# The adaLN sums of a two-layer trunk block: from VectorE and TensorE to ScalarE and GpSimd

## The chip, the core and the metric

The kernel runs on one NeuronCore of a Trainium2 chip. The metric is the device time of one execution in microseconds (us). TensorE is PE in the rows, its weight loads PEld, VectorE is DVE, ScalarE is ACT, GpSimd is POOL, and SyncE is SP, which issues all the loads.

## The reference, cut to what matters

Two trunk layers, each with a mixer sub-layer (two attentions and a pooling branch) and a squared-ReLU MLP, run on 256 latent and 256 context tokens of width 1024. Each layer takes its shifts, scales and gates from two conditioning vectors:

```python
def modulate(x, g, shift, scale):
    return rmsnorm(x, g) * (1 + scale) + shift

def adaln(v, w, b):
    m = jax.nn.silu(v) @ w + b          # v: 1024, w: 1024 x 6144
    return jnp.split(m, 6, axis=-1)     # shift, scale, gate of each sub-layer
...
x = x + g1 * merge(oa, ob, oc, ga, gb, gc, w_br_a[l], w_br_b[l], w_br_c[l], w_out[l])
x = x + g2 * mlp(modulate(x, norm2[l], sh2, sc2), w_mlp1[l], w_mlp2[l])
```

The change concerns the product `silu(v) @ w` alone. Layer 0 needs it for both vectors; layer 1 needs it for both in the first norm and for the latents' vector alone after that.

## The kernel before

All numbers are float32. To keep their precision on TensorE, every operand is split into a high part (a cast on ScalarE) and a low part (a subtraction on VectorE), and a product takes three matmuls (`mm3`). The weights come as pieces `st` of 128 x 1024 values; `halves` turns a piece into `wh` and `wl`, each in one of four buffers (`W_HL_BUFS`), ahead of its use. Each engine runs its own queue of instructions in a fixed order. The order comes from a planner: cooperative threads (`_Flow`) emit the program, and a table of assumed costs (`_Engine`, `_TensorEngine`) tells each thread when to go on.

The first norm's shift and scale in layer 0 are made on TensorE at the start (`First`), and the change leaves that alone. The other adaLN sums are a background thread, `ada_all`. It walks over groups of 512 of the 6144 columns. For each group `ada_acc` loads eight 128 x 512 tiles of the weights (`sta`, two tiles to a load) and, for each vector, multiplies each tile by a silu column `s_col` (one value per partition) and adds it to an accumulator `acc`. This is one instruction on VectorE for each tile and vector. What is left is a sum over the 128 partitions, for 32 accumulators in all:

- shift and scale (`ada_cols_end`, 20 accumulators): four transposes on TensorE into the tile `act`, then a reduction on VectorE gives columns (`mod`);
- gates (`ada_rows_end`, 12 accumulators): `acc` is split into `ach` and `acl`, two matmuls with a matrix of ones give the sum on every partition (`ar`), and VectorE adds it to the loaded bias `grow`.

GpSimd has little to do before: the powers of the norms (`rstd`, `qr`, `rsqA`, `rsqC`), the rotary tables `tab` and a few memsets.

Of the kernel before, what the change touches and what calls it, by code (L numbers as in the profile page):

```python
# [9 lines left out]
F32R = mybir.dt.float32r  # L10
AF = mybir.ActivationFunctionType
# [4 lines left out]
P = 128  # L16
# [18 lines left out]
ADA_PAUSE = 0.8  # L35
# [8 lines left out]
ADA_SLACK = 10.0  # L44
# [7 lines left out]
# order in which the layers take the chunks of w_in (see _layout)  # L52
# [6 lines left out]
# the loads of the start: token tiles, halves of the first norm's shift and scale, halves of the first chunks  # L59
# [11 lines left out]
class _Event:  # L71
    """A point of the program whose results other threads wait for."""
# [5 lines left out]
class _Engine:  # L78
    """An engine whose instructions advance the flow's estimate of its time table."""
# [58 lines left out]
class _TensorEngine:  # L138
# [6 lines left out]
    def _step(self, out, lhsT, rhs, size, transpose=False):  # L145
        """the array's clock is full in a tick after one with enough columns, else half"""
# [27 lines left out]
class _Flow:  # L174
    """Cooperative threads that emit the program in the order in which the tensor engine should run it.

    A thread yields None (it can go on at once), a time (it can go on then) or an event."""
# [26 lines left out]
    def ready(self, *aps, eng=None):  # L204
        """when an engine sees the last write to these regions"""
# [21 lines left out]
    def held(self, pool):  # L227
        """how many tiles of a pool are in use"""
# [4 lines left out]
    def free(self, *aps):  # L233
        """the last uses of these tiles are in the program"""
# [8 lines left out]
    def room(self, pool, n, most):  # L243
        """wait until n more tiles of a pool fit"""
# [44 lines left out]
# priorities of the threads, the lowest number first  # L289
# [4 lines left out]
def kernel(ctx: ExitStack, tc: tile.TileContext, a: dict, out: bass.AP):  # L294
# [55 lines left out]
    def stage(src, nk, ncol):  # L350
        """a load of at most 1024 columns, on its way"""
# [14 lines left out]
    def halves(v, nk, ncol):  # L366
        """(hi, lo) of a staged load's rows"""
# [13 lines left out]
    class Chunk:  # L381
        """the (hi, lo) pairs of a chunk's rows, in two pieces"""
# [12 lines left out]
        def used(self, k):  # L395
            """row k is not needed any more, nor are those before"""
# [3 lines left out]
    class Stream:  # L400
        """Chunks of weights [128, nk, ncol], each staged in two loads and split ahead of its use"""
# [24 lines left out]
        def next(self):  # L426
            """the next chunk"""
# [5 lines left out]
    def mm3(ps, lh, rh, start, stop):  # L433
        """ps (+)= (lh_hi + lh_lo)^T (rh_hi + rh_lo), without lo * lo"""
# [13 lines left out]
    class Pair:  # L448
        """a (hi, lo) pair of tiles that some thread is going to write"""
# [19 lines left out]
    def reload_x():  # L469
        """the stream's input for the first residual sum"""  # L470
# [14 lines left out]
    # silu(c) as columns: 0.5 c (1 + tanh(c / 2))  # L485
# [9 lines left out]
    # adds the (hi, lo) rows of both vectors  # L495
# [14 lines left out]
    def finish_mod(l, which, vec, half):  # L510
        """A = norm (1 + scale), B = shift as per-partition columns"""
# [5 lines left out]
    class First:  # L517
        """half of the columns of shift and scale of layer 0, norm 1, both vectors, on the tensor engine"""
# [6 lines left out]
        def row(self, typ, kk, w):  # L525
            """one of the eight row tiles of one type: rows (hi, lo) x vectors"""
# [37 lines left out]
    def ada_acc(l, j, vecs, accs):  # L564
        """per-partition partial sums of silu(c) @ w_ada[:, 512 j : 512 j + 512]"""
# [4 lines left out]
        nxt = yield from fetch(0)  # L570
        for h in range(4):
# [4 lines left out]
            if h == 0:  # L576
                yield from fl.room("b", len(vecs), B_BUFS - ADA_SPARE)
# [1340 lines left out]
```

## Time and profile before

| | before |
|---|---|
| median of 3 runs (lowest to highest) | 1159.73 us (1159.59 to 1160.59) |
| the profiled execution, its span | 1159.7 us |
| PE busy | 1138.5 us, 98% |
| DVE busy | 872.7 us, 75% |
| ACT busy | 636.2 us, 55% |
| POOL busy | 70.7 us, 6%, 84 instructions |

Busy time is the time in which an engine has an instruction running, over the whole span. A share near 100% says that the engine hardly ever waited; a low share says nothing of the moments in which others waited for that engine.

### The profile page before, as it was taken

The page shows a single profiled execution, that of the slowest core. Times are in us where ns is not written, and L with a number is a line of the kernel's source. Part 1 is how long each engine was busy: PE and PEld are TensorE (multiplying, and loading weights), DVE is VectorE, ACT ScalarE, POOL GpSimd, SP SyncE. Part 2 cuts the span into 40 slices and gives each one's busy share as a digit, 9 for nine tenths or more (in the row PEclk, how much of TensorE's full clock was granted, in tenths as well). Part 3 has the DMA queues.
Part 4 walks back from the last instruction along what each step waited for, and adds up shares of the span by engine and source line. Part 5 has one row for each costly group of instructions (what it writes and reads, how often), then busy time and mean ns, then how long its engine had stood idle before and what let it go on. Part 6 is the DMA issues. An engine that isn't in the chain of part 4 may idle for free.

```text
span 1159.7 us, 17946 instructions
## 1 busy us (share of the span) xinstructions
PE 1138.5 (98%) x6636; PEld 998.0 (86%) x6636; DVE 872.7 (75%) x1653; ACT 636.2 (55%) x1356; POOL 70.7 (6%) x84
## 2 busy tenths in 40 slices
PE   5999999999999999999999999989999999999998
PEld 2898889888888898888888888889999998999886
DVE  5878989889888679878677634689777885987453
ACT  6867786664633564321133323576877865666332
POOL 0224001100000000000000000023002000000000
PEclk9899999999999999999999999999999999999999
DMA  8752235243435435556655423554334471775562
GB/s 308 271 166 97 85 105 188 90 153 121 136 137 178 138 119 178 180 180 214 213 178 185 163 92 107 166 168 153 103 128 137 155 241 40 269 238 183 192 216 75
DMA packets 59992, 186.85 MB, mean 161 GB/s; under 512 B 7296, under 2 KB 8064, under 8 KB 59904
## 3 DMA queue, kind: packets, MB, share of 16 engines
q1 hardware_dynamic: 59904, 185.71, 47.8%
q8 instruction: 52, 0.85, 0.3%
q14 instruction: 36, 0.29, 0.1%
HBM read 184.63 MB, written 1.05 MB: 160 GB/s over the span
## 4 chain that ended last, share of the span: by engine, by line
PE 95%; DMA 2%; ACT 2%; DVE 1%; SPq 0%; issue 0%; POOL 0%; DVEq 0%; POOLq 0%
PE tm L167 28%; PE h L167 23%; PE g L167 17%; PE qkv L167 8%; PE br L167 6%; PE sc L167 3%; PE po L167 2%; PE pT L171 2%; PE u L167 1%; DMA ad<-in_wada_dram 1%; PE xT L171 1%; PE ada L167 1%; PE act L171 1%; PE qT L171 1%; PE kT L171 1%; ACT hh L133 1%
## 5 line engine op out<-in xcount | busy, mean ns | idle before, releaser
L133 DVE TENSOR_TENSOR wl<-st,wh 128x1024 fp32r<-128x1024 f32 x216 | 263.6, 1223 | 133.7 <-ACT wh L133 133.1
L133 ACT CAST wh<-st 128x1024 fp32r<-128x1024 f32 x216 | 227.9, 1058 | 231.8 <-PE tm L167 151.2
L167 PE MATMUL h<-hh,wh 128*128 128x256 f32 (+1 forms) x736 | 186.7, 316 | 0.0
L167 PE MATMUL h<-hh,wl 128*128 128x256 f32 (+1 forms) x512 | 168.8, 330 | 0.2 <-DVE wl L133 0.2
L133 DVE SCALAR_TENSOR_TENSOR acc<-sta,s_col,acc 128x512 f32<-128x512 f32 x224 | 159.3, 743 | 3.0 <-DMA sta<-in_wada_dram 2.4
L167 PE MATMUL tm<-wh,ah 128*128 128x512 f32 x384 | 150.3, 391 | 0.0
L167 PE MATMUL tm<-wl,ah 128*128 128x512 f32 x384 | 149.5, 389 | 0.0
L167 PE MATMUL tm<-wh,al 128*128 128x512 f32 x384 | 149.5, 389 | 0.0
L167 PE MATMUL g<-hh,wh 128*128 128x512 f32 (+1 forms) x384 | 132.6, 345 | 0.0
L167 PEld LDWEIGHTS h<-hh,wh 128*128 128x128 f32 x736 | 124.1, 190 | 8.8
L167 PE MATMUL g<-hl,wh 128*128 128x512 f32 (+1 forms) x384 | 129.3, 337 | 0.0
L167 PE MATMUL g<-hh,wl 128*128 128x512 f32 (+1 forms) x384 | 129.3, 337 | 0.0
L167 PE MATMUL h<-hl,wh 128*128 128x512 f32 (+1 forms) x288 | 105.4, 366 | 0.1
L167 PEld LDWEIGHTS h<-hh,wl 128*128 128x128 f32 x512 | 97.0, 190 | 9.3 <-DVE wl L133 0.5
L167 PEld LDWEIGHTS tm<-wh,al 128*128 128x128 f32 x384 | 72.1, 188 | 15.2
L167 PEld LDWEIGHTS tm<-wl,ah 128*128 128x128 f32 x384 | 72.1, 188 | 14.7
L167 PEld LDWEIGHTS tm<-wh,ah 128*128 128x128 f32 x384 | 72.1, 188 | 14.5
L167 PE MATMUL qkv<-wh,hh 128*128 128x256 f32 x272 | 79.7, 293 | 1.1 <-ACT hh L133 1.1
L167 PE MATMUL qkv<-wl,hh 128*128 128x256 f32 x272 | 79.0, 290 | 1.8 <-DVE wl L133 1.8
L167 PEld LDWEIGHTS g<-hh,wl 128*128 128x128 f32 x384 | 72.8, 190 | 8.0
L167 PE MATMUL qkv<-wh,hl 128*128 128x256 f32 x272 | 79.1, 291 | 0.1
L167 PEld LDWEIGHTS g<-hh,wh 128*128 128x128 f32 x384 | 72.8, 190 | 6.7 <-ACT p L133 0.3
(188 smaller groups left out, 2178.6 us busy)
## 6 DMA issues: line engine op xcount, KB each, us to landing
st<-in_w_dram SPq DMA_DIRECT2D x136, 512.0 KB, 4.5
sta<-in_wada_dram SPq DMA_DIRECT2D x80, 512.0 KB, 4.1
st<-in_win_dram SPq DMA_DIRECT2D x72, 512.0 KB, 4.6
ad<-in_wada_dram SPq DMA_DIRECT2D x32, 256.0 KB, 7.1
st<-in_wout_dram SPq DMA_DIRECT2D x8, 512.0 KB, 5.5
wor<-in_wout_dram SPq DMA_DIRECT2D x16, 256.0 KB, 4.9
grow<-in_b_ada_dram SPq DMA_DIRECT2D x12, 256.0 KB, 5.1
kr<-in_wbr_a_dram SPq DMA_DIRECT2D x12, 256.0 KB, 5.0
```

What stands on the lines that cost most here:

```text
L133: return fn(*args, **kw)
L167: return self._e.matmul(out, lhsT, rhs, start=start, stop=stop)
L171: return self._e.transpose(out, in_, identity)
```

## The change

The adaLN partial sums move. For each tile and vector ScalarE multiplies the tile by the silu column into a tile `part` (the first one straight into `acc`), and GpSimd adds `part` to `acc`. There are two `part` tiles for each vector of a group, used in turn. The sum over partitions becomes one GpSimd instruction, `partition_all_reduce`, which leaves the total on every partition (`tot`). For columns GpSimd then multiplies `tot` by the identity and VectorE reduces each row of the product to one value; for gates GpSimd adds `tot` to the bias. The factor 0.5 of one gate moves into the residual sum. The thread waits for ScalarE's and GpSimd's planned queues instead of VectorE's, and `calm_way` waits at most 12 planned us. The rest of the diff takes out comments and docstrings and is not shown.

```diff
-ADA_PAUSE = 0.8
+ADA_DEPTH = 3.0
...
+            if op == "partition_all_reduce":
+                per, cost = 6.3e-3, 0.4
...
-        while self.norms:
+        end = self.now + 12.0
+        while self.norms and self.now < end:
             yield self.now + 0.1
...
             if h == 0:
-                yield from fl.room("b", len(vecs), B_BUFS - ADA_SPARE)
+                yield from fl.room("b", 3 * len(vecs), B_BUFS - ADA_SPARE)
                 accs.extend(tmp(s="acc") for _ in vecs)
+                for i in range(2):
+                    parts[i] = [tmp(s="part") for _ in vecs]
             for k in range(2):
                 kk = 2 * h + k
-                yield from V.calm(ADA_CALM[l])
+                yield from S.calm(ADA_CALM[l])
+                yield from G.calm(ADA_DEPTH)
                 yield from fl.calm_way()
-                for acc, vec in zip(accs, vecs):
-                    sc = s_col[:, kk, vec : vec + 1]
-                    if kk == 0:
-                        V.tensor_scalar(out=acc, in0=st[:, k], scalar1=sc, scalar2=None, op0=ALU.mult)
-                    else:
-                        V.scalar_tensor_tensor(out=acc, in0=st[:, k], scalar=sc, in1=acc, op0=ALU.mult, op1=ALU.add)
+                to = parts[kk % 2] if kk else accs
+                for part, vec in zip(to, vecs):
+                    S.activation(part, st[:, k], AF.Copy, scale=s_col[:, kk, vec : vec + 1])
                 if k:
                     free(st)
-                yield fl.ready(*accs) + ADA_PAUSE
+                if kk:
+                    for acc, part in zip(accs, to):
+                        yield fl.ready(part)
+                        G.tensor_tensor(out=acc, in0=acc, in1=part, op=ALU.add)
+        free(*[q for r in parts.values() for q in r])
...
+    def ada_sum(acc):
+
+        yield fl.ready(acc)
+        yield from fl.calm_way()
+        yield from fl.room("b", 1, B_BUFS - ADA_SPARE)
+        tot = tmp(s="tot")
+        G.partition_all_reduce(tot, acc, P, ReduceOp.add)
+        yield fl.ready(tot)
+        return tot
+
     def ada_cols_end(l, which, vecs, half, typ, accs, left):
...
-            yield from banks(1, 2)
-            pt = bank("act")
-            for i in range(4):
-                PE.transpose(pt[:, i * P : (i + 1) * P], acc[:, i * P : (i + 1) * P], ident)
-            yield fl.ready(pt)
+            tot = yield from ada_sum(acc)
+
+            dg = acc.rearrange("p (i q) -> p i q", i=4)
+            G.tensor_tensor(out=dg, in0=tot.rearrange("p (i q) -> p i q", i=4), in1=ident.unsqueeze(1).to_broadcast([P, 4, P]), op=ALU.mult)
+            free(tot)
+            yield fl.ready(acc)
+            yield from V.calm(ADA_CALM[l])
             dst = mods[l][:, 2 * which + typ, vec, half * 4 : half * 4 + 4]
-            V.tensor_reduce(out=dst, in_=pt.rearrange("p (i q) -> p i q", i=4), axis=AX.X, op=ALU.add)
+            V.tensor_reduce(out=dst, in_=dg, axis=AX.X, op=ALU.add)
...
-        for (ah, al), vec, g in zip(hl, vecs, gs):
-            yield from banks(1, 2)
-            ps = bank("ar")
-            PE.matmul(ps, ones, ah, start=True, stop=False)
-            PE.matmul(ps, ones, al, start=False, stop=True)
...
+        for acc, vec, g in zip(accs, vecs, gs):
+            tot = yield from ada_sum(acc)
+            free(acc)
+            yield fl.ready(g)
+            G.tensor_tensor(out=g, in0=g, in1=tot, op=ALU.add)
+            free(tot)
```

The change also moves instructions in the fixed orders. GpSimd's queue in the attention of layer 0 held only the powers of the query and key norms before:

```order
L133 TENSOR_TENSOR rsqA_179<-rsqA_179,neg_half 128x4 x2
L133 TENSOR_TENSOR rsqA_179<-rsqA_179,neg_half 128x2
L133 TENSOR_TENSOR rsqC_180<-rsqC_180,neg_half 128x2
L133 TENSOR_TENSOR rsqA_179<-rsqA_179,neg_half 128x2
L133 TENSOR_TENSOR rsqC_180<-rsqC_180,neg_half 128x2
L133 TENSOR_TENSOR qr_2428<-qr_2428,neg_half 128x2
```

At the same place, GpSimd's queue of the changed program ends the first two accumulators of a gate:

```order
L135 TENSOR_TENSOR rsqC_172<-rsqC_172,neg_half 128x2
L135 TENSOR_TENSOR acc_766<-acc_766,part_768 128x512
L135 TENSOR_TENSOR acc_767<-acc_767,part_769 128x512
L135 TENSOR_TENSOR acc_766<-acc_766,part_770 128x512
L135 TENSOR_TENSOR acc_767<-acc_767,part_771 128x512
L135 ISA
L135 ISA tot_1533<-acc_766 128x512
L135 ISA
L135 TENSOR_TENSOR grow_1523<-grow_1523,tot_1533 128x512
L135 ISA
L135 ISA tot_1608<-acc_767 128x512
L135 ISA
```

The row that writes `tot` is the sum over partitions. The ISA rows without operands are not in the source: the built program names each one a reload of a library index, 1 ahead of the sum and 0 behind it. Over the whole program there are 32 sums and 61 reloads, one of which (index 0, ahead of the mask that makes `ident`) stands in the program before as well.

ScalarE's queue in the MLP of layer 0 held casts of the weights (`wh`) and the activations of the hidden units before:

```order
L133 ACTIVATE relu_5608<-h_1299_5550 128x512
L133 ACTIVATE ah_5618<-relu_5608 128x512
L133 CAST wh_5629<-st_5479 128x1024
L133 CAST wh_5650<-st_5541 128x1024
L133 ACTIVATE relu_5658<-h_1308_5604 128x512
L133 ACTIVATE ah_5663<-relu_5658 128x512
```

Now products for the adaLN sums stand between them:

```order
L135 ACTIVATE part_5558<-sta_5583,s_col 128x512
L135 ACTIVATE part_5559<-sta_5583,s_col 128x512
L135 ACTIVATE relu_5692<-h_1320_5645 128x512
L135 ACTIVATE ah_5697<-relu_5692 128x512
L135 ACTIVATE part_5560<-sta_5583,s_col 128x512
L135 ACTIVATE part_5561<-sta_5583,s_col 128x512
L135 CAST wh_5712<-st_5549 128x1024
L135 CAST wh_5732<-st_5637 128x1024
```

The tiles `part_5558` to `part_5561` belong to one group and are written again and again in turn, so each write stands behind GpSimd's add that read the tile's last content.

## Rows read from the trace of the kernel before

**Rows 1.** The page, part 1: busy us, share of the span, instructions.
```profile
PE 1138.5 (98%) x6636; PEld 998.0 (86%) x6636; DVE 872.7 (75%) x1653; ACT 636.2 (55%) x1356; POOL 70.7 (6%) x84
```

**Rows 2.** The page, part 4: the chain that ended last, by engine.
```profile
PE 95%; DMA 2%; ACT 2%; DVE 1%; SPq 0%; issue 0%; POOL 0%; DVEq 0%; POOLq 0%
```

**Rows 3.** Three stretches: busy us (count) of PE, PEld, DVE, ACT, POOL; clock, DMA share, GB/s.
```profile
0.00:107.00 107.00, 94.89 (x562) 76.30 (x563) 82.86 (x215) 75.69 (x220) 29.23 (x42) 0.95 0.66 226
107.00:606.00 499.00, 498.68 (x2620) 426.22 (x2620) 413.50 (x753) 247.39 (x507) 12.01 (x12) 1.00 0.45 150
606.00:1160.00 554.00, 544.94 (x3458) 495.50 (x3456) 376.30 (x687) 313.15 (x629) 29.45 (x30) 1.00 0.48 158
```

**Rows 4.** Groups by line and shape: TensorE's adaLN work. xcount | busy us, mean ns
```profile
L171 PE MATMUL act<-ident,acc 128*128 128x128 f32 x80 | 12.0, 272 | 0.0
...
L167 PE MATMUL ar<-ach,ones1.0_112 128*128 128x512 f32 x6 | 2.4, 396 | 0.0
...
L167 PE MATMUL ar<-acl,ones1.0_112 128*128 128x512 f32 x6 | 2.4, 392 | 0.0
```

**Rows 5.** The same view: VectorE's adaLN sums, a ScalarE product of the same size.
```profile
L133 DVE SCALAR_TENSOR_TENSOR acc<-sta,s_col,acc 128x512 f32<-128x512 f32 x224 | 159.3, 743 | 3.0 <-DMA sta<-in_wada_dram 2.4
...
L133 ACT ACTIVATE p<-p,den 128x512 f32<-128x512 f32 x48 | 32.5, 736 | 0.3 <-DVE den L133 0.3
```

**Rows 6.** Timeline of POOL at the start: start us, us, instruction.
```profile
0.73 0.20 POOL masks.py:197 MEMSET ident<- 128x128 f32 x1 [0.29 <-POOLq L1907]
1.01 0.29 POOL masks.py:199 TENSOR_SCALAR_AFFINE_SELECT ident<-ident 128x128 f32<-128x128 f32 x1
1.39 0.19 POOL L133 TENSOR_TENSOR pair_sum<-ident 128x2 f32<-128x2 f32 x1
```

**Rows 7.** The rotary tables' tile: ns of one, lowest/median/highest.
```profile
L133 POOL TENSOR_TENSOR tab<-rope,gains x8: 717/918/1717, 44.3 to 766.3; 128x256 f32<-128x256 f32 x8
```

**Rows 8.** Timelines of DVE and POOL about the two runs of table instructions.
```profile
43.30 0.88 DVE L133 TENSOR_SCALAR xh<-st,rstd 128x512 f32<-128x512 f32 x2 [0.44 <-POOL rstd L133]
44.27 3.69 POOL L133 TENSOR_TENSOR tab<-rope,gains 128x256 f32<-128x256 f32 x4 [1.00 <-DMA gains<-in_gains_dram]
47.38 0.17 DVE L133 TENSOR_TENSOR mod<-adat,b_col 128x8 f32<-128x8 f32 x1 [2.06 <-PE adat L167]
...
762.75 1.22 DVE L133 TENSOR_TENSOR wl<-st,wh 128x1024 fp32r<-128x1024 f32 x1
763.22 4.79 POOL L133 TENSOR_TENSOR tab<-rope,gains 128x256 f32<-128x256 f32 x4
763.89 1.84 DVE L133 TENSOR_SCALAR xh<-x,rstd 128x512 f32<-128x512 f32 x2
765.65 1.75 DVE L133 TENSOR_TENSOR wl<-st,wh 128x1024 fp32r<-128x1024 f32 x1
```

**Rows 9.** Timeline of POOL: powers of one and of four columns.
```profile
9.05 0.55 POOL L133 TENSOR_TENSOR rstd<-rstd,neg_half 128x1 f32<-128x1 f32 x1 [7.15 <-DVE rstd L133]
74.77 1.01 POOL L133 TENSOR_TENSOR rsqA<-rsqA,neg_half 128x4 f32<-128x4 f32 x1 [7.32 <-ACT v L133]
```

**Rows 10.** DMA issues: KB of one, us from issue to landing.
```profile
ad<-in_wada_dram SPq DMA_DIRECT2D x32, 256.0 KB, 7.1
...
gains<-in_gains_dram SPq DMA_DIRECT2D x1, 256.0 KB, 6.6
...
s_raw<-in_cc_dram SPq DMA_DIRECT2D x1, 8.0 KB, 1.6
...
sink<-in_sink_dram SPq DMA_DIRECT2D x1, 6.0 KB, 6.0
pscale<-in_pscale_dram SPq DMA_DIRECT2D x1, 2.0 KB, 5.4
```

**Rows 11.** Who waited for whom: us in total, times, longest us.
```profile
ACT wh L133 <- PE tm L167: 151.2, 55, 9.0
```

**Rows 12.** Groups by line and shape: one matmul of the MLP's second product.
```profile
L167 PE MATMUL tm<-wh,ah 128*128 128x512 f32 x384 | 150.3, 391 | 0.0
```

More of the change, by code (lines that the diff above doesn't have):

```diff
@@ L5 @@
 from concourse import mybir
+from concourse.bass_isa import ReduceOp
 from concourse.masks import make_identity
@@ L43 @@
 MAIN_SPARE = (1, 0)
-ADA_SLACK = 10.0
 BR_SPARE = (4, 8)
@@ L570, in ada_acc @@
         nxt = yield from fetch(0)
+        parts = {}
         for h in range(4):
@@ L627, with ada_rows @@
             rows_ev[l, i] = _Event()
-    def ada_rows(l, idx, vecs, ones, factor):
+    def ada_rows(l, idx, vecs):
         left = [0, 1]
@@ L634, in ada_rows, with ada_rows_end @@
             yield from ada_acc(l, idx * 2 + half, vecs, accs)
-            fl.spawn(ada_rows_end(l, idx, vecs, ones, factor, half, accs, left), P_ADA)
-    def ada_rows_end(l, idx, vecs, ones, factor, half, accs, left):
+            fl.spawn(ada_rows_end(l, idx, vecs, half, accs, left), P_ADA)
+    def ada_rows_end(l, idx, vecs, half, accs, left):
         yield from fl.room("grow", len(vecs), GROW_BUFS)
@@ L645, in ada_rows_end @@
             load(g, a["b_ada"][l : l + 1, c0 : c0 + 512].to_broadcast([P, 512]))
-        hl = []
-        yield from fl.room("b", 2 * len(accs), B_BUFS - ADA_SPARE)
-        for acc in accs:
-            yield from fl.calm_way()
-            ah, al = tmp(F32R, "ach"), tmp(F32R, "acl")
-            yield from hilo_steps(acc, ah, al)
-            hl.append((ah, al))
-            free(acc)
-        yield fl.ready(*[q for p in hl for q in p]) + ADA_SLACK
-        for (ah, al), vec, g in zip(hl, vecs, gs):
-            yield from banks(1, 2)
-            ps = bank("ar")
-            PE.matmul(ps, ones, ah, start=True, stop=False)
-            PE.matmul(ps, ones, al, start=False, stop=True)
-            free(ah, al)
-            yield fl.ready(g, ps)
-            yield from fl.calm_way()
-            V.scalar_tensor_tensor(out=g, in0=g, scalar=factor, in1=ps, op0=ALU.mult, op1=ALU.add)
-            free(ps)
+        for acc, vec, g in zip(accs, vecs, gs):
+            tot = yield from ada_sum(acc)
+            free(acc)
+            yield fl.ready(g)
+            G.tensor_tensor(out=g, in0=g, in1=tot, op=ALU.add)
+            free(tot)
             rows[l, idx][vec][half] = g
@@ L675 @@
     S.copy(out=identr, in_=ident)
-    ones = {}
-    for f in (0.5, 1.0):
-        of = half(s="ones")
-        G.memset(of[:, :P], f)
-        ones[f] = const([P, P], F32R, f"ones{f}")
-        S.copy(out=ones[f], in_=of[:, :P])
-        free(of)
     rope = const([P, 2, 2, HD], F32, "rope")
@@ L1494, in to_residual @@
             for c in cs:
-                V.tensor_tensor(out=tm[:, c], in0=rows[l, idx][t // 2][n][:, c], in1=ps[:, c], op=ALU.mult)
+                row = rows[l, idx][t // 2][n][:, c]
+                if idx == 2:
+                    V.scalar_tensor_tensor(out=tm[:, c], in0=row, scalar=0.5, in1=ps[:, c], op0=ALU.mult, op1=ALU.mult)
+                else:
+                    V.tensor_tensor(out=tm[:, c], in0=row, in1=ps[:, c], op=ALU.mult)
             free(ps)
@@ L1758, in ada_all @@
         yield layer_started[0]
-        yield from ada_rows(0, 2, (0, 1), ones[0.5], 0.5)
+        yield from ada_rows(0, 2, (0, 1))
         yield from ada_cols(0, 1, (0, 1))
-        yield from ada_rows(0, 5, (0, 1), ones[1.0], 1.0)
+        yield from ada_rows(0, 5, (0, 1))
         yield from ada_cols(1, 0, (0, 1))
         yield from ada_cols(1, 1, (0,))
-        yield from ada_rows(1, 2, (0,), ones[0.5], 0.5)
+        yield from ada_rows(1, 2, (0,))
         yield mlp_started[1]
-        yield from ada_rows(1, 5, (0,), ones[1.0], 1.0)
+        yield from ada_rows(1, 5, (0,))
     layer_started = [_Event()]
```

2 lines of the change are left out of this document (removed).

## The prediction, as it went on record

> **What bounds the kernel now.** I read the page's busy shares first: TensorE is busy for 98% of the span, VectorE for 75%, ScalarE for 55%, GpSimd for 6% [rows 1]. The chain that ended last then says whether the busy engine is also the one that sets the end: 95% of it is TensorE, and GpSimd is 0% [rows 2]. The three stretches show where that holds. Between 107 and 606 us TensorE is busy for 498.68 of 499 us at a granted clock of 1.00, its higher level of 2.4 GHz, while ScalarE is busy for 247 and GpSimd for 12 us [rows 3]. So an instruction taken from TensorE's queue there shortens the kernel by its own duration, and work given to ScalarE or GpSimd costs nothing until TensorE has to wait for it. The question of this change is therefore whether GpSimd, which waits for nothing important now, becomes something that others wait for.
>
> **What it removes.** TensorE loses 80 transposes, 12.0 us, and four groups of six matmuls with ones, 2.4 us each, of which two are shown: 9.6 us [rows 4]. Together that is 21.6 us on the engine that sets the end. VectorE loses 224 multiply-adds, 159.3 us [rows 5], and some small work. VectorE's loss itself buys little: TensorE was hardly waiting [rows 3].
>
> **What it adds on ScalarE.** 256 products of 128 x 512. The nearest row is a product of that size with one factor for each partition, 736 ns [rows 5], so 256 x 0.736 = 188 us, 224 of them (165 us) between 107 and 606 us. There ScalarE goes from 247 to about 410 of 499 us. That fits beside TensorE, so I cost it at nothing; if the cover is gone, it is because ScalarE waits and not because it works (below).
>
> **What it adds on GpSimd.** To place it, I count the matmuls that stand ahead of a GpSimd instruction in the changed program, leave the adaLN's own out, and look up when the trace of before had run as many. By that count the first sum over partitions stands at 107 us, and the last add of the long run of groups at 606 us. Between them stand 216 adds and multiplies into `acc`, 8 adds into `grow`, 28 sums over partitions, 52 library reloads and 12 powers. Each price:
>
> - An add of 128 x 512. An add of 128 x 2 takes 0.19 us [rows 6], a product of 128 x 256 at best 0.717 and in the middle 0.918 us [rows 7]. A straight line through 2 and 256 columns gives 1.25 us from the lowest and 1.65 us from the middle one for 512 columns. I take 1.4 us, since a part of the adds will run undisturbed. The disturbed case is in the trace: four table products took 3.69 us where VectorE sat idle for 2.06 us of the time, and 4.79 us beside a `wl` subtraction and two `xh` products, and there VectorE lost too: the `xh` pair took 1.84 us where it had taken 0.88, and a `wl` took 1.75 us where the one before took 1.22 [rows 8]. The bounds are 1.25 and 1.75 us. The Trainium skill (SBUF — State Buffer, Who interferes with whom) says why: a GpSimd instruction and a VectorE instruction with two SBUF inputs lock each other out, one waiting until the other ends. The trace agrees in direction.
> - A sum over partitions of 128 x 512. The trace has none. It has to read and write as much as an add, so at least 1.25 us. I take three times that, 3.75 us, for reading, adding across and handing the total back; this is an estimate that no row supports beyond its lower end. The upper end, the price of a power, is a rival below.
> - A library reload. The trace has one, at the start, where the library is already in place: between the memset that ends at 0.93 us and the mask that starts at 1.01 us there is next to nothing [rows 6]. That is the lower bound, about 0.1 us. In the changed program each reload asks for another library than the one before, so something has to be fetched. The nearest rows for a fetch are single loads: 1.6 us for the smallest in an idle start, 5.4, 6.0 and 6.6 us for the one-off loads of constants, 7.1 us for the first weights [rows 10]. I take the middle one of the constants, 6.0 us, and 7.1 us as the upper bound. The Trainium skill (GPSIMD Engine Reference, Instruction dispatch) puts the first call after such a load at about 6 us and says that the profile shows no instruction for it; no run here shows that yet, and by it the sum would be the same.
> - A power takes 0.55 us for one column and 1.01 us for four [rows 9]; I take 0.9 us.
>
> Sum between the two places: 224 x 1.4 = 314, 28 x 3.75 = 105, 52 x 6.0 = 312 and 12 x 0.9 = 11, that is 742 us of work in the time in which TensorE goes through 499 us. GpSimd ends some 243 us late.
>
> **Who waits for it.** ScalarE first. A group has two `part` tiles for each vector, so ScalarE's product of the fourth tile must wait for GpSimd's add of the second. Behind that product in ScalarE's queue stand the casts `wh` and the activations `relu`, and TensorE waits for those. VectorE's reduction into `mod` waits for GpSimd's last multiply, with the subtractions `wl` behind it. So GpSimd's lateness reaches TensorE through both engines, less what is ready ahead. That reserve I read from the weights: `wh` has four buffers, and ScalarE waited 55 times for TensorE to free one, at longest 9.0 us [rows 11]. One piece feeds 24 matmuls of 391 ns [rows 12], 9.4 us; three pieces ahead are 28 us. In the attentions less is ready ahead, so 28 us is the most that is hidden. In the stretch paced by GpSimd the matmuls removed buy nothing. After 606 us 4 transposes and 8 matmuls with ones are still gone, 4 us; the four sums that follow there have hundreds of us around them.
>
> Sum, against the profiled execution's 1159.7 us (its span, which is also the median of the runs to 0.1 us): 1159.7 + 243 - 28 - 4 = **1371 us**.
>
> **The rivals.**
>
> 1. *The reloads are free.* If they cost 0.1 us, as the one at the start does [rows 6], GpSimd has 314 + 105 + 5 + 11 = 435 us of work in 499 us. It is late only here and there, by no more than the 28 us in reserve, and the 21.6 us leave TensorE's queue: 1159.7 - 21.6 = 1138 us, or up to 1150 if ScalarE, at 410 of 499 us, is late in the attentions. For it speaks the only reload in the trace; against it, that this one had nothing to fetch. It decides below 64 us for 52 reloads, about 1.3 us each. Chance 0.12.
> 2. *A reload is a short fetch.* At 2 us, near the smallest load, the work is 314 + 105 + 104 + 11 = 534 us, 35 us over; less 28 that is 7, and more where GpSimd sat idle early and could not use the time: 1160 to 1200 us, within 0.2% at the lower end. For it speaks the 1.6 us row; against it, that the loads of constants, small ones among them, took 5.4 to 6.6 us [rows 10]. Chance 0.11.
> 3. *The sum over partitions is slow for each column, as a power is.* From one to four columns a power grows by 0.46 us [rows 9], 0.153 us a column, 78 us for 512. Then 32 sums are 2,500 us, and with the 741 - 105 us of the rest GpSimd alone is busy for over 3,100 us; after the last sum, which stands at 1020 us, some 140 us of TensorE's work follow. That gives about 3,350 us. The Trainium skill (GPSIMD Engine Reference, Cross-partition — where GPSIMD wins) measures the partition-axis `tensor_reduce` at 247,699 ns for 2048 columns; an estimate from it is 62 us for 512 columns, or 1,980 us for 32, which would also leave GpSimd as the bound. It is another instruction, and no run here shows either. For the rival speaks that powers show GpSimd capable of such prices; against it, that a sum is only additions, and plain adds are the cheap rows. Chance 0.06.
> 4. *Forecast:* reloads cost as much as a load from memory does, GpSimd paces the middle of the kernel. Chance 0.71.
>
> **How the numbers follow.** Within the forecast the bounds move the sum so: reloads at 5.4 us take 31 off, at 7.1 us add 57; adds at 1.25 us take 34 off, at 1.75 us add 78; the sum over partitions at 1.25 us takes 70 off. Not all ends come together: its own range is 1290 to 1470 us. The range to be held 8 times in 10 leaves out the free reloads (0.12) and the slow sums (0.06), so it reaches down to the short fetch: 1165 to 1470 us. A measurement of this kernel can tell about 0.2% from no change. Faster by more than that: rival 1, 0.12. Within it: the lower end of rival 2, 0.02. Slower: 0.86.
>
> **What would show it.** In the changed profile, between the reload and the sum POOL's timeline should have gaps of several us ahead of each sum and of the add behind it, while TensorE's busy share between 107 and some 840 us falls to about two thirds. The waits should name ScalarE's `part` waiting for POOL's `acc`, and DVE's `mod` waiting for POOL's `acc`, some 200 us in total on ScalarE. The `act` and `ar` rows are gone; a ScalarE product `part` should read about 0.74 us and a GpSimd add 1.25 to 1.75 us. From the last add of the long run on, the timeline should be that of before, shifted. The prediction is wrong if the gaps about the sums are under 1.3 us, if the sums themselves take tens of us, or if ScalarE waits and TensorE does not, which would mean that far more is ready ahead than the four weight buffers.

## The result and the profile after

The changed kernel takes 1540.6 us, the median of four runs (1532.1 to 1543.7), against 1159.7 us: a ratio of 1.327, 95% interval 1.3235 to 1.3308. It is slower by 381 us. The prediction had the direction and the bottleneck, but forecast only 211 us more, and the time lies above its range.

The page of the changed kernel, part 1 (busy us, share of the span, instructions), and part 4 (the chain that ended last, by engine), against [rows 1, 2]:

```profile
PE 1205.8 (78%) x6532; PEld 1032.1 (67%) x6532; DVE 820.1 (53%) x1373; ACT 785.8 (51%) x1598; POOL 533.7 (35%) x370
...
PE 47%; issue 24%; POOL 11%; DVE 7%; ACT 7%; DMA 3%; SPq 0%; POOLq 0%; DVEq 0%; ACTq 0%
```

No engine is busy for more than 78% of the span, and TensorE's part of the chain fell from 95% to 47%. The largest newcomer, with 24%, is "issue": time in which an engine waited for nothing that the profile shows. Whose time that is, the timeline of POOL tells (start us, us, instruction, idle time before it):

```profile
106.29 2.87 POOL L135 TENSOR_TENSOR acc<-acc,part 128x512 f32<-128x512 f32 x2
114.67 3.25 POOL L135 PARTITION_ALL_REDUCE tot<-acc  x1 [5.50 <-issue]
125.01 1.27 POOL L135 TENSOR_TENSOR grow<-grow,tot 128x512 f32<-128x512 f32 x1 [7.10 <-issue]
...
590.95 1.25 POOL L135 TENSOR_TENSOR acc<-tot,ident 128x512 f32<-128x512 f32 x1 [7.35 <-DMA st<-in_w_dram]
598.24 6.92 POOL L135 PARTITION_ALL_REDUCE tot<-acc  x2 [6.04 <-issue]
613.16 1.33 POOL L135 TENSOR_TENSOR grow<-grow,tot 128x512 f32<-128x512 f32 x1 [7.99 <-issue]
```

In these rows 5.5 and 6.0 us without an instruction stand ahead of a sum over partitions, and 7.1 to 8.0 us behind it; over the whole kernel the medians are 6.1 and 7.2 us, and the longest 9.2 and 8.0 us. At 598 us two sums stand back to back, and there is no gap between them. So the gap belongs to the change of instruction, which is where the program has its library reloads, and not to the sum. There are 60 such gaps, about 198.9 us ahead of the sums and 219.5 us behind them, 6.97 us each. The Trainium skill (GPSIMD Engine Reference, Instruction dispatch) puts the first call after a load at about 6 us, with no instruction in the profile; the trace agrees on both, with a somewhat larger figure.

The groups of the page (busy us, mean ns of one | idle before), against [rows 5, 7]:

```profile
L135 POOL TENSOR_TENSOR acc<-acc,part 128x512 f32<-128x512 f32 x224 | 327.3, 1482 | 186.5 <-issue 109.5
L135 ACT ACTIVATE part<-sta,s_col 128x512 f32<-128x512 f32 x224 | 155.5, 722 | 311.7 <-POOL acc L135 303.9
...
L135 POOL PARTITION_ALL_REDUCE tot<-acc x32 | 104.4, 3268 | 198.9 <-issue 141.9
...
L135 DVE TENSOR_REDUCE mod<-acc 128x4 f32<-128x512 f32 x20 | 13.7, 685 | 224.4 <-POOL acc L135 224.4
```

An add takes 1.48 us, a product 0.72 us, and a sum over partitions 3.27 us, where 3.75 us had been a guess. The waits name both roads to TensorE (us in total, times, longest), against [rows 11]:

```profile
ACT part L135 <- POOL acc L135: 303.9, 71, 22.5
...
DVE mod L135 <- POOL acc L135: 224.4, 18, 19.9
...
ACT wh L135 <- PE tm L169: 75.8, 37, 4.4
...
POOL acc L135 <- ACT part L135: 74.3, 22, 13.2
PE tm L169 <- ACT wh L135: 72.3, 9, 18.6
PE h L169 <- ACT wh L135: 72.3, 6, 22.2
```

ScalarE waits for GpSimd with the casts `wh` behind it, and TensorE waits for `wh`, which it did not do before. VectorE waits for GpSimd too. The fourth row shows that the waiting goes round: GpSimd waits for ScalarE's products as well.

The stretches: the place that stood at 606 us before, counted in TensorE's matmuls without the adaLN's own, is reached 953 us into the span; the last add of the long run ends at 956 us (columns as in [rows 3]).

```profile
0.00:107.00 107.00, 93.89 (x568) 75.05 (x568) 84.47 (x203) 85.30 (x235) 40.86 (x53) 0.97 0.67 227
107.00:953.00 846.00, 562.80 (x2520) 458.95 (x2521) 366.35 (x526) 379.48 (x720) 422.57 (x265) 0.81 0.28 93
953.00:1540.00 587.00, 549.08 (x3445) 498.09 (x3444) 369.29 (x646) 321.01 (x645) 70.29 (x54) 0.97 0.44 143
```

The middle takes 846 us where it took 499: 347 of the 381 us. The first stretch is unchanged, and the last is 33 us longer. GpSimd is busy for 423 us of the middle; the 52 reloads there take 52 x 6.97 = 362 us more. Together that is 785 us, and some 61 us are left in which GpSimd did nothing. By the timeline of POOL, 48 us of that are waits for ScalarE's products and most of the rest waits for VectorE ahead of a power. The longest run of them stands early:

```profile
161.57 2.54 POOL L135 TENSOR_TENSOR acc<-acc,part 128x512 f32<-128x512 f32 x2 [6.23 <-ACT part L135]
170.56 2.53 POOL L135 TENSOR_TENSOR acc<-acc,part 128x512 f32<-128x512 f32 x2 [6.45 <-ACT part L135]
180.30 2.54 POOL L135 TENSOR_TENSOR acc<-acc,part 128x512 f32<-128x512 f32 x2 [7.21 <-ACT part L135]
```

TensorE did not wait there: it was busy for all of the 39 us from 147 to 186 us. TensorE is busy for 67% of the whole stretch.

### The profile page after: what moved, and what is told of

It is laid out like the page before. It is cut to its first block, busy times and chain, and to the rows that moved or that the text cites. A ratio compares the mean times of both kernels' runs of the same rounds, so it can differ in the third digit from the quotient of the medians.

```text
span 1540.3 us, 18393 instructions
## 1 busy us (share of the span) xinstructions
PE 1205.8 (78%) x6532; PEld 1032.1 (67%) x6532; DVE 820.1 (53%) x1373; ACT 785.8 (51%) x1598; POOL 533.7 (35%) x370
## 4 chain that ended last, share of the span: by engine, by line
PE 47%; issue 24%; POOL 11%; DVE 7%; ACT 7%; DMA 3%; SPq 0%; POOLq 0%; DVEq 0%; ACTq 0%
PE tm L169 13%; PE h L169 12%; PE g L169 7%; POOL acc L135 6%; PE qkv L169 5%; POOL tot L135 5%; PE br L169 3%; DVE wl L135 2%; ACT wh L135 2%; PE po L169 2%; ACT p L135 2%; ACT part L135 1%; PE u L169 1%; PE pT L173 1%; PE sc L169 1%
## 5 line engine op out<-in xcount | busy, mean ns | idle before, releaser
L135 DVE TENSOR_TENSOR wl<-st,wh 128x1024 fp32r<-128x1024 f32 x216 | 292.7, 1361 | 200.4 <-ACT wh L135 200.2
L135 POOL TENSOR_TENSOR acc<-acc,part 128x512 f32<-128x512 f32 x224 | 327.3, 1482 | 186.5 <-issue 109.5
L135 ACT ACTIVATE part<-sta,s_col 128x512 f32<-128x512 f32 x224 | 155.5, 722 | 311.7 <-POOL acc L135 303.9
L169 PE MATMUL h<-hh,wh 128*128 128x256 f32 (+1 forms) x736 | 196.9, 330 | 72.3 <-ACT wh L135 72.3
L169 PE MATMUL h<-hh,wl 128*128 128x256 f32 (+1 forms) x512 | 177.4, 347 | 15.0 <-DVE wl L135 14.9
L169 PEld LDWEIGHTS h<-hh,wh 128*128 128x128 f32 x736 | 131.5, 201 | 83.8 <-ACT wh L135 74.6
L135 POOL PARTITION_ALL_REDUCE tot<-acc x32 | 104.4, 3268 | 198.9 <-issue 141.9
L135 DVE TENSOR_REDUCE mod<-acc 128x4 f32<-128x512 f32 x20 | 13.7, 685 | 224.4 <-POOL acc L135 224.4
L169 PE MATMUL h<-hl,wh 128*128 128x512 f32 (+1 forms) x288 | 111.9, 389 | 9.3 <-DVE hl L135 9.3
L135 POOL TENSOR_TENSOR rstd<-rstd,neg_half 128x1 f32<-128x1 f32 x14 | 10.0, 714 | 298.4 <-DVE rstd L135 298.3
```

The lines of the kernel that those rows point to most:

```text
L135: return fn(*args, **kw)
L169: return self._e.matmul(out, lhsT, rhs, start=start, stop=stop)
```

## The experiments

Two questions stood open: how the 381 us divide among reloads, adds, products and waits, and why GpSimd, which paces the middle, was idle there for 61 us. All times are medians, each with its ratio to the kernel before, run on the same chip, and the 95% interval.

| kernel | us | ratio | interval |
|---|---|---|---|
| the change | 1540.6 | 1.327 | 1.3235 to 1.3308 |
| no reloads (e1) | 1238.5 | 1.068 | 1.0661 to 1.0693 |
| sums on TensorE (e2) | 1203.0 | 1.038 | 1.0356 to 1.0410 |
| sums on GpSimd alone (e3) | 1361.0 | 1.174 | 1.1709 to 1.1771 |
| sums in pairs (e4) | 1416.3 | 1.222 | 1.2198 to 1.2250 |
| e2, four `part` tiles (e5) | 1209.6 | 1.043 | 1.0410 to 1.0445 |
| e2, adds on VectorE (e6) | 1171.7 | 1.010 | 1.0089 to 1.0119 |
| before, idle adds on GpSimd (e7) | 1301.6 | 1.122 | 1.1198 to 1.1243 |
| the change, four `part` tiles (e8) | 1561.4 | 1.346 | 1.3428 to 1.3481 |
| the change, sums priced (e9) | 1347.4 | 1.162 | 1.1584 to 1.1647 |
| pairs, sums priced (e10) | 1304.8 | 1.125 | 1.1226 to 1.1282 |
| the change, later reductions (e11) | 1472.5 | 1.269 | 1.2673 to 1.2713 |
| groups of up to four, priced (e12) | 1276.9 | 1.101 | 1.0996 to 1.1033 |

### What each part costs: e1, e2, e3, e6

**e1** replaces each sum over partitions by three adds of its size, so no library changes; the sum over partitions is left out:

```diff
-        G.partition_all_reduce(tot, acc, P, ReduceOp.add)
+        for _ in range(3):
+            G.tensor_tensor(out=tot, in0=acc, in1=acc, op=ALU.add)
```

> The changed kernel with each sum over partitions replaced by three adds of the same size on GpSimd (the sum over partitions is left out). GpSimd's work stays about the same (3 x 1.25 us for 3.27 us), but no library reload is left except the one at the start. Theory (the reloads, about 7 us each, pace GpSimd and through it ScalarE, VectorE and TensorE): 1135 to 1160 us, GpSimd late by no more than the reserve. First rival (the adds on GpSimd and their lock-outs with VectorE are what is slow): over 1300 us, since all adds are still there. Second rival (ScalarE's products, waiting for part tiles two deep, block its queue whatever the sums cost): over 1250 us.

The time, 1238 us, lies between the theory and both rivals: 302 of the 381 us go with the reloads, but 79 us stay, where the theory had allowed none. GpSimd is busy for 584.5 us, 51 us more than in the change, so it is not less work on it that saved the time. The page's groups show that GpSimd keeps its adds, at 1.58 us each now:

```profile
L135 POOL TENSOR_TENSOR acc<-acc,part 128x512 f32<-128x512 f32 x224 | 347.7, 1575 | 112.5 <-ACT part L135 109.8
```

**e2** keeps products and adds as changed and leaves the sums on TensorE, as before. Against the kernel before only the accumulation differs, with the planner's waits that belong to it:

```diff
-                        V.scalar_tensor_tensor(out=acc, in0=st[:, k], scalar=sc, in1=acc, op0=ALU.mult, op1=ALU.add)
...
+                    S.activation(part, st[:, k], AF.Copy, scale=s_col[:, kk, vec : vec + 1])
...
+                        G.tensor_tensor(out=acc, in0=acc, in1=part, op=ALU.add)
```

> Only the first half of the change: ScalarE's products and GpSimd's adds as in the changed kernel, the sums over partitions on TensorE and VectorE as in the kernel before. No reload, no sum on GpSimd, and TensorE has its 21.6 us back. Theory (reloads): 1150 to 1170 us, about the time before. Both rivals: over 1250 us, since the adds and the two-deep part tiles are unchanged.

Neither theory nor rival: 1203 us. With no sum and no reload left on GpSimd (it is busy for 415.6 us in all) the products and adds still cost 43 us.

**e6** is e2 with the adds on VectorE:

```diff
-                yield from G.calm(ADA_DEPTH)
+                yield from V.calm(ADA_CALM[l])
...
-                        G.tensor_tensor(out=acc, in0=acc, in1=part, op=ALU.add)
+                        V.tensor_tensor(out=acc, in0=acc, in1=part, op=ALU.add)
```

> The first half of the change alone, with the 224 adds on VectorE in place of GpSimd; ScalarE's products stay. GpSimd is as idle as before. If the 44 us come from GpSimd (its adds, the lock-outs, or the powers queued behind them): 1155 to 1170 us. If they come from ScalarE's 185 us of added work: 1195 to 1210 us.

It takes 1171.7 us, 2 us above the first case: 31 of e2's 43 us come with GpSimd as the place of the adds, and 12 with ScalarE's products and what else e2 and e6 share. VectorE's subtractions `wl` show the difference too: one takes 1.37 us in e2, and 1.22 us in e6 as in the kernel before (e7, below, looks at this alone). This is the version nearest to the kernel before, and none was faster.

**e3** is the other half: VectorE multiplies and accumulates as before, and GpSimd does the sums. Against the change:

```diff
-                    S.activation(part, st[:, k], AF.Copy, scale=s_col[:, kk, vec : vec + 1])
...
-                        G.tensor_tensor(out=acc, in0=acc, in1=part, op=ALU.add)
+                        V.scalar_tensor_tensor(out=acc, in0=st[:, k], scalar=sc, in1=acc, op0=ALU.mult, op1=ALU.add)
```

> Only the second half of the change: VectorE multiplies and adds up as in the kernel before, GpSimd sums over partitions, with 64 reloads between. GpSimd has 32 x (3.3 + 1.3) us and 64 x 7 us, 595 us in all and some 490 us of it in the 499 us between 107 and 606 us, and ScalarE no longer waits for it. Theory: VectorE's reduction still waits for GpSimd with the wl subtractions behind it, and the two sums ahead of layer 1's queries still delay the first powers there: 1200 to 1320 us. First rival (adds) and second rival (part tiles): neither is left, so 1135 to 1150 us.

At 1361 us it is slower than the upper end of the theory. The sums alone, with 64 gaps, cost 201 us although GpSimd has no adds of partial products. The waits show how:

```profile
DVE mod L136 <- POOL acc L136: 199.1, 19, 42.1
ACT wh L136 <- PE tm L170: 170.3, 52, 32.7
POOL tot L136 <- DVE acc L136: 169.2, 12, 30.9
```

VectorE's reduction waits for GpSimd, and behind it in VectorE's queue stand the multiply-adds for the next sum, for which GpSimd then waits.

### Fewer reloads: e4

Two sums stand together, then their two users:

```diff
-        tot = tmp(s="tot")
-        G.partition_all_reduce(tot, acc, P, ReduceOp.add)
+        tots = [tmp(s="tot") for _ in accs]
+        for tot, acc in zip(tots, accs):
+            G.partition_all_reduce(tot, acc, P, ReduceOp.add)
```

> The changed kernel, but the two sums of a group stand back to back, so that a pair needs one reload ahead and one behind: 38 reloads in place of 60, all else as it was. Theory: 22 reloads at 7.0 us are gone, 154 us: 1370 to 1410 us. Both rivals: unchanged, 1520 to 1545 us.

38 gaps in place of 60, and 124 us less, 5.7 us for each reload that went: 1416 us, 6 us above the theory and far below the rivals. Together with e1 this shows that, in this order of instructions, the reloads carry most of the loss, at 5 to 6 of their 7 us.

### Deeper tiles, idle adds: e5, e8, e7

**e5** and **e8** give e2 and the changed kernel four `part` tiles for each vector:

```diff
-                yield from fl.room("b", 3 * len(vecs), B_BUFS - ADA_SPARE)
+                yield from fl.room("b", 5 * len(vecs), B_BUFS - ADA_SPARE)
...
-                for i in range(2):
+                for i in range(4):
...
-                to = parts[kk % 2] if kk else accs
+                to = parts[kk % 4] if kk else accs
```

> The first half of the change alone (sums over partitions on TensorE), with four part tiles for each vector in place of two. It took 1203 us with two. If the remaining 44 us come from ScalarE's products waiting for part tiles (32 us of such waits in that run): 1165 to 1180 us. If they come from ScalarE's added work, or from VectorE and GpSimd locking each other out: 1195 to 1205 us.

> The changed kernel with four part tiles for each vector in place of two. In the stretch that GpSimd paces, its own work (796 us by the measured prices) and its waits for ScalarE's products (some 55 us) add up to the 849 us that the stretch took. If those waits come from the two-deep part tiles: 1480 to 1510 us. If the reloads alone count and ScalarE finds its products in time in any case: 1530 to 1545 us.

Both came out a little slower (by 7 and 21 us), beyond either expectation. In e8 the wait only changes sides:

```profile
DVE mod L135 <- POOL acc L135: 313.8, 19, 22.3
ACT part L135 <- POOL acc L135: 196.0, 33, 34.6
POOL acc L135 <- ACT part L135: 188.4, 24, 66.7
```

ScalarE waits 108 us less and VectorE 89 us more, and GpSimd waits 188 us for ScalarE's products, not 74. So more tiles did not end GpSimd's idle time. The test is not a clean one: with four tiles the planner moved the groups as well. e8 has 64 gaps in place of 60, and 20 sums in place of 28 stand ahead of the place that had been 606 us, which it reaches at 853 us and not at 953; the rest comes later.

**e7** is the kernel before, plus 224 GpSimd adds that nobody reads, one behind each of VectorE's multiply-adds (and, not shown, 40 memsets of their tiles, 20.4 us):

```diff
                         V.scalar_tensor_tensor(out=acc, in0=st[:, k], scalar=sc, in1=acc, op0=ALU.mult, op1=ALU.add)
+                        G.tensor_tensor(out=idle[0], in0=idle[0], in1=idle[1], op=ALU.add)
```

> The kernel before, unchanged in all that it computes, plus 224 adds of 128 x 512 on GpSimd whose result nobody reads, one behind each multiply-add of VectorE. No engine waits for them except the powers that are queued behind them. If lock-outs between VectorE and GpSimd (and the powers' place in the queue) are what the 44 us are: 1185 to 1210 us. If not: 1157 to 1163 us.

It is 142 us slower, far above both. VectorE's groups between 107 us and the same place (733 us here), and then the same groups of the kernel before between 107 and 606 us:

```profile
L133 DVE SCALAR_TENSOR_TENSOR acc<-sta,s_col,acc 128x512 f32<-128x512 f32 x190 | 197.5, 1077 | 4.3 <-DMA sta<-in_wada_dram 3.9
L133 DVE TENSOR_TENSOR ptl<-pT,pth 128x512 fp32r<-128x512 f32 x36 | 24.1, 679 | 12.8 <-ACT pth L133 12.8
L133 DVE TENSOR_TENSOR al<-sq,ah 128x512 fp32r<-128x512 f32 x18 | 21.1, 1170 | 1.1
```

```profile
L133 DVE SCALAR_TENSOR_TENSOR acc<-sta,s_col,acc 128x512 f32<-128x512 f32 x186 | 131.4, 743 | 2.0 <-DMA sta<-in_wada_dram 1.4
L133 DVE TENSOR_TENSOR ptl<-pT,pth 128x512 fp32r<-128x512 f32 x36 | 24.0, 682 | 5.9 <-ACT pth L133 5.8
L133 DVE TENSOR_TENSOR al<-sq,ah 128x512 fp32r<-128x512 f32 x19 | 13.0, 686 | 1.2 <-DVE sq L133 0.5
```

VectorE's instructions with two inputs in SBUF got longer, 0.743 to 1.077 us and 0.686 to 1.170 us. One that reads a PSUM tile (`ptl<-pT`) did not, 0.682 to 0.679 us. That is the rule of the Trainium skill (SBUF — State Buffer, Who interferes with whom): a VectorE instruction with two SBUF inputs and a GpSimd instruction that reads SBUF lock each other out of the ports that they share. Two inputs are not the only case: the first multiply of a group, `acc<-sta,s_col`, reads one SBUF tile and a column, and it went from 0.478 to 1.060 us. The `xh` products of [rows 8], which the prediction put under that rule, are of this kind too. VectorE is busy for 583 of 626 us there, where it had been busy for 414 of 499 us. It stands idle for 43 us in place of 85, so it is its longer instructions, and not waits for the powers, that fill the added time. The theory was right in kind and wrong in size. In the changed kernel itself VectorE no longer has the multiply-adds, so this price falls on fewer instructions.

### Where the waiting instructions stand: e9 to e12

The planner counts 3.6 us for a sum over partitions (0.4 us and 6.3 ns a column) and nothing for a reload; on the chip a sum with its two reloads takes 17.2 us. **e9** gives the planner that price and changes nothing else:

```diff
             if op == "partition_all_reduce":
-                per, cost = 6.3e-3, 0.4
+                per, cost = 6.3e-3, 14.4
```

> The changed kernel, whose planner now counts 14.4 us on top of the per-column cost for a sum over partitions (two gaps of about 7 us each), where it counted 0.4: nothing is computed differently, only the places of the instructions in the queues move. Theory: some 53 us in the long stretch (GpSimd waits there for ScalarE's products) and some 34 us behind it come from instructions that the planner writes too early, VectorE's reductions and ScalarE's products, which block their queues until GpSimd gets there. Then GpSimd's own work of about 796 us takes the place of the 849 us, and the late sums stop no one: 1455 to 1490 us. Rival: the idle time is the price of the fetch chain or of the two engines taking turns, whatever is written where: 1530 to 1550 us.

It takes 1347 us. That is 193 us less than the change and 108 us below the lower end of what the theory gave. The waits that the theory named did shrink: ScalarE's for GpSimd from 303.9 to 88.2 us and VectorE's from 224.4 to 74.7 us. But the number of gaps did not fall, it is 62, and what moved is the work itself. GpSimd's multiplies of `tot` in the changed kernel and, below, in e9 (ns, lowest/median/highest; first and last start):

```profile
L135 POOL TENSOR_TENSOR acc<-tot,ident x20: 1251/1258/2267, 275.1 to 934.3; 128x512 f32<-128x512 f32 x20
```

```profile
L135 POOL TENSOR_TENSOR acc<-tot,ident x20: 1251/1294/2289, 282.0 to 1052.6; 128x512 f32<-128x512 f32 x20
```

The last of the 20 column sums starts at 1053 us, although the kernel is shorter. By then e9 is only 142 us behind the kernel before, so this is about place 910, while 934 us is about place 595 in the changed kernel. 28 sums stood ahead of place 606, and about 19 do now; that TensorE passes the place 220 us sooner shows that the others were not needed that early. GpSimd's load ahead of place 606 falls, by e9's windows:

```profile
107.00:733.00 626.00, 502.05 (x2521) 425.71 (x2518) 340.38 (x505) 338.74 (x654) 294.32 (x186) 0.89 0.31 103
```

It is busy for 294 us (423 in the changed kernel) and has 38 gaps, about 274 us (362): 217 us less, and the stretch is 220 us shorter. GpSimd still does nothing for some 58 of the 626 us, as before. The theory had the right lever and the wrong mechanism: the idle time did not go away, the deadline did. What is left waits at a real deadline, the second norm of layer 0. Timelines of DVE and PE in e9:

```profile
456.06 0.58 PE L169 MATMUL h<-hh,wh 128*128 128x256 f32 x1 [28.80 <-ACT hh L135]
...
475.74 0.69 DVE L135 TENSOR_REDUCE mod<-acc 128x4 f32<-128x512 f32 x1 [30.68 <-POOL acc L135]
...
494.48 0.58 PE L169 MATMUL h<-hl,wh 128*128 128x256 f32 x1 [37.84 <-DVE hl L135]
```

TensorE loses 37.8 us there, and 28.8 us just before, at 456 us: it waits for the normed inputs `hh` and `hl` of the MLP, whose shift and scale are still in GpSimd's queue.

**e11** moves VectorE's reduction alone, 20 us by the planner's clock:

```diff
-            yield fl.ready(acc)
+            yield fl.ready(acc) + 20.0
             yield from V.calm(ADA_CALM[l])
             dst = mods[l][:, 2 * which + typ, vec, half * 4 : half * 4 + 4]
```

> The changed kernel with one thing moved: VectorE's reduction of a masked sum is written 20 us later by the planner's clock, so that it stands behind more of VectorE's other work; ScalarE's products and GpSimd's work stay as they are. If VectorE's wait for GpSimd (224 us in the changed kernel) is part of what holds TensorE beyond GpSimd's own work: 1480 to 1515 us, and VectorE's wait falls below 100 us. If ScalarE's wait (304 us) alone does it: 1530 to 1550 us, with VectorE's wait down and ScalarE's not.

1472 us, a little better than the theory asked, and the wait fell from 224 to 19 us:

```profile
DVE mod L135 <- POOL acc L135: 18.8, 2, 13.4
```

But ScalarE's wait stayed (288 us), and so did GpSimd's idle time: in the stretch up to the same place GpSimd is busy for 389 of 746 us and has 42 gaps and the start of another (298 us), which leaves 59 us, about as in the changed kernel. The stretch is shorter because ten gaps and 34 us of work are no longer in it. Not all of that went behind place 606: the whole kernel has 54 gaps in place of 60, since more sums stand back to back. So GpSimd's queue did change with the later reductions, and six gaps fewer are part of the 68 us. VectorE's wait was not what kept GpSimd idle, and it had cost less than its 224 us look like.

**e10** is e4 with the same price, and **e12** puts up to four sums together (those of shift and scale of a half), each priced at 3.9 us, and else is as e10:

```diff
-            for typ in range(2):
-                accs = []
-                yield from ada_acc(l, (3 * which + typ) * 2 + half, vecs, accs)
-                fl.spawn(ada_cols_end(l, which, vecs, half, typ, accs, left), P_ADA)
+            both = []
+            for typ in range(2):
+                accs = []
+                yield from ada_acc(l, (3 * which + typ) * 2 + half, vecs, accs)
+                both.append(accs)
+            fl.spawn(ada_cols_end(l, which, vecs, half, both), P_ADA)
```

> The kernel with the sums in pairs (38 switches in place of 60; it took 1416 us) with the same price of 14.4 us a sum in the planner. Theory (places in the queues): 1330 to 1380 us. Rival: 1405 to 1425 us.

> Sums of the shift and scale columns in groups of four (those of the gate rows in twos or alone, as they are finished): 28 switches in place of the 40 of the kernel with pairs and a price, and the planner counts 3.9 us beside the per-column cost of each sum, which is what two gaps of 7 us come to over four. All else is as in that kernel. Theory (with the places priced, the time goes with the switches that are left; from 62 to 40 of them took 42.6 us, 1.9 us each): 1270 to 1295 us. Rival (what is left is the sharing between engines and GpSimd's adds, which stay): 1300 to 1320 us. Second rival (the reductions, priced lower again, stand too early once more): over 1330 us.

e10 takes 1305 us with 40 gaps, 25 us below the theory's range and 100 us below the rival's; e12 takes 1277 us with 26 gaps (28 had been expected), inside its theory's range. From 62 to 40 gaps the time falls by 1.9 us a gap, from 40 to 26 by 2.0 us (the second step changes the planner's price of a sum too, so it is not the gaps alone). Without the price a gap cost 5.0 us (e1, 302 us over 60) or 5.7 us (e4). So a reload of 7 us costs the kernel most of its length where the order makes the others wait, and about 2 us where it mostly runs beside them. Carried on to no gap at all, e12's line ends at 1277 - 26 x 2 = 1225 us, an estimate that lies between e1 and e2. Of the 117 us that e12 still loses, the gaps would be 52 us by that line, and e2's products and adds 43 us.

## Why the prediction was right and wrong

**Right.** GpSimd became the bound between places 107 and 606 us, through ScalarE's `part` and VectorE's `mod`, as predicted. Nearly every price holds: 423 us for GpSimd's instructions against 430 (adds 1.48 for 1.4 us, sums 3.27 for 3.75 us; the two misses cancel in part, which is luck), the product 0.72 for 0.74 us, no gap between two sums, and TensorE busy for two thirds of the stretch. ScalarE's wait for GpSimd was 304 us and not some 200. Rivals 1 to 3 fell with the gaps of 7 us and the sums of 3.3 us.

The price of a reload was taken from loads of constants, and it came out near. That a reload is such a load is not shown: the instruction queues of the page (part 3) moved 88 packets before and 92 after, for 60 reloads more, so the profile has no fetch for them. The nearness may be luck. Two of the readings slipped without moving the forecast. The load of 1.6 us is the shortest of [rows 10] but not the smallest: `pscale`, with 2 KB against 8, took 5.4 us, which speaks against rival 2 more than was said. And the room for free reloads in rival 1 is 499 - 430 = 69 us, not 64.

**Wrong.** Four terms of the sum 1159.7 + 243 - 28 - 4 were off:

- *Reloads at 6.0 us.* They took 6.97 us, 52 of them 50 us more. With the other prices 7 us lower, GpSimd's work was 785 us where the sum had 742: +43 us. This was within the bounds given.
- *The 499 us as GpSimd's time, with no wait of its own.* The sum treated GpSimd as never waiting once it is late. It did nothing for some 61 us of the stretch, 48 us of them while it waited for ScalarE's products: +61 us.
- *The reserve of 28 us.* Next to nothing of it is seen. TensorE's shift at place 606 is 347 us, the whole of 846 - 499, where the sum had 215: +28 us. TensorE reached the place at 953 us and the last add of the run ended at 956 us, so TensorE was some 3 us ahead of GpSimd and not 28. Why the weight pieces gave no more, no run shows.
- *The late sums with "hundreds of us around them"*, -4 us. They cost +34 us. The first two share GpSimd's queue with the powers of layer 1, as POOL's timeline shows:

```profile
1138.90 3.25 POOL L135 PARTITION_ALL_REDUCE tot<-acc  x1 [5.98 <-ACT stk L135]
1149.67 1.25 POOL L135 TENSOR_TENSOR grow<-grow,tot 128x512 f32<-128x512 f32 x1 [7.53 <-issue]
1150.90 2.05 POOL L135 TENSOR_TENSOR rsqA<-rsqA,neg_half 128x4 f32<-128x4 f32 x2
1152.92 0.69 POOL L135 TENSOR_TENSOR qr<-qr,neg_half 128x2 f32<-128x2 f32 x1
```

The power `qr` of a query norm stands behind two sums and four reloads. VectorE waited 19.9 us for it and TensorE 15.7 us for VectorE, and the shift grows there from 346 to 363 us. At the third late sum, 1375 us into the span, it grows from 368 to 381 us: a product of ScalarE waited 12.7 us for the add behind that sum, a cast `wh` stood behind the product, and TensorE waited 9.2 us for `wh`. What was asked of the late sums was who needs their result; the question left out was what stands behind them in their queue.

These four add up to the miss: 43 + 61 + 28 + 38 = 170 us, 381 less 211. This is bookkeeping on one trace, not an experiment for each term. The first was a size; the second to fourth were steps that assumed an engine with slack around its waits.

**Where the 381 us come from.** By the experiments: 12 us with ScalarE's products (e6 against before), 31 us more with adds on GpSimd (e2 against e6), 35 us more with the sums' plain work there (e1 against e2), and 302 us with the reloads (the change against e1). These shares depend on the order in which the parts are added: alone, the first half of the change costs 43 us (e2) and the second 201 us (e3), 244 together, so some 137 of the 381 us arise only where both share GpSimd's queue. Of the 302, e9 gives 193 back without taking one reload away. So the greater part of what the reloads cost goes back to a planner that knows nothing of them and writes the sums, and the engines' uses of them, far ahead of need. This changes none of the prices above; it explains why they could all fall on the path.

**Open.** GpSimd's idle time of about 60 us in the stretch stands in the changed kernel, e9 and e11 alike. The timelines name it: waits for ScalarE's products are 48 of 62 us in the changed kernel, 50 of 58 in e9 and 52 of 59 in e11. Deeper `part` tiles (e8) and later reductions (e11) did not end it, though both moved GpSimd's work as well. In the changed kernel ScalarE itself was busy for 45 of those 48 us, so the products stood behind its other work and not behind casts that waited for TensorE. No run wrote them earlier in ScalarE's queue, so what that would give stays open.

## What to carry over

When work goes to an engine that was idle, add up its whole queue, gaps between instructions included, over the stretch in which the others need it, and take no slack off that no row shows: 3 of the assumed 28 us showed, and the engine that paced the stretch also waited. Keep kinds of GpSimd instructions apart in groups, and tell whoever writes the order what a change between them costs: the first took the kernel from 1347 to 1277 us, the second from 1541 to 1347 us. Before moving an operation to a helper engine, ask what stands behind it in that engine's queue, and not only who needs its result.

## What the runs showed of the hardware

- A change between `partition_all_reduce` and the other GpSimd instructions costs about 6 us ahead of the sum and about 7 us behind it, and shows as idle time whose releaser is "issue". Where another event happens to fall into the gap, the profile names that one: the gap of 7.35 us at 591 us in the first timeline above carries a DMA's name.
- The sum over partitions of 128 x 512 is steady: lowest 3246 and median 3247 ns of 32 (mean 3268). That is two to three plain adds at 1.25 us, and far from the 78 us that the price of a power for each column would make [rows 9].
- 224 adds that nobody reads, on an engine that was idle, made the kernel 12% slower (e7), because they lengthened VectorE's instructions with two SBUF inputs, and one with a single SBUF tile, `acc<-sta,s_col`, from 0.478 to 1.060 us. The one that reads a PSUM tile, `ptl<-pT,pth`, kept its 0.68 us.
- In the stretch that GpSimd paces, the mean granted clock of TensorE is 0.81, a mix of its two levels of 1.2 and 2.4 GHz, where it had been 1.00 without pauses [rows 3]. TensorE is busy for 563 us there with work that took it 481 us before (499 less the adaLN's own 18). What that adds to the kernel's time, beside the waits, no run separates.
